# Pairs of column tiles of the input projection as seven products of halves, with sums of weights kept from the first block

## The chip, the core and the metric

The kernel runs on one core of one Trainium2 chip. The metric is the device time of one launch in microseconds. A core has TensorE (matmuls, PE in the rows; its weight loads are PEld), VectorE (DVE), ScalarE (ACT), GpSimd (POOL), and SyncE (SP), which here issues the DMAs. Each engine works through its own queue in order.

## What is computed

One layer of a decoder trunk on 2048 tokens of 1024 channels. The four branches read the same normalised rows `h` through one projection of 9992 columns:

```python
h = _rmsnorm(x, norm_pre)
cols = h @ w_in
(dn_qkv, dn_z, dn_b, dn_a, gm_uv, gm_z, sw_q, sw_k, sw_v, sw_z,
 xm_q, xm_z, gate_logits) = _split_cols(cols)
mem_kv = _rmsnorm(mem, norm_mem) @ w_mem_kv
y_a = _deltanet_branch(dn_qkv, dn_z, dn_b, dn_a, conv_w, a_log, dt_bias, dn_norm)
y_b = _spatial_gating_branch(gm_uv, gm_z, gm_norm, spatial_w, spatial_b)
y_c = _sliding_window_branch(sw_q, sw_k, sw_v, sw_z, sinks)
y_m = _memory_branch(xm_q, xm_z, mem_kv)
proj = jnp.einsum("btnc,ncd->btnd", jnp.stack([y_a, y_b, y_c, y_m], axis=2), w_up)
gates = jax.nn.sigmoid(gate_logits.reshape(B, T, N_BRANCH, D))
out = jnp.sum(gates * proj, axis=2) @ w_out
return x + _rmsnorm(out, norm_post)
```

## The kernel before

**Tiles.** The 2048 tokens go in four blocks of 512 (`NPASS` is 4, a block is a pass `p` of the main loop). A block's `h` is held transposed, channels on the partitions: `hhi` and `hlo`, each 8 row tiles of 128 channels by 512 tokens. To keep float32 precision every operand is split in two: `hi` is the value cast to the matmul's type, `lo` is the rest, and `mac3` (L258) adds hi·hi, lo·hi and hi·lo into PSUM, three matmuls per row tile.

**Projection.** `proj2` (L264) makes two column tiles of 128 columns for the 512 tokens of a block: for each half `j` of the 1024 channels `wunit` (L228) loads 128 x 1024 weights (512 KB), splits them in two halves of 128 x 512 (ScalarE casts `hi`, L249; VectorE or GpSimd subtracts `lo`, L250, by the list `ON_DVE` and a count of three), and 24 matmuls of 512 columns follow. Two PSUM banks of the four under the tag `mm` take the pair, and `done` reads each bank. The columns of one block are 37 such pairs: `dn` (delta net q, k, v; names dn0, dn1, dnv), `gu` and `gz`, `skv`, `sq` and `sz`, `xq` and `xz`, `az`, and 16 `gate` pairs. The values `gv` and the output `wo` go with tokens on the partitions (`tokmajor`).

**Gates and up-projections.** `gates_up` (L422) makes for each of four branches and four pairs the gate's pair, then two up-projections of 4 x 3 matmuls, and adds their product to `merged` (VectorE L454, GpSimd L455). Where `h` is 1024 channels, an up-projection has 512.

**Order.** The main loop runs a foreground generator (`fg`) and after each of its steps one step of each background generator in `bg`: the convolutions, the delta rule's chain (`dn_step`, `dn_scan`; two a block), the sliding-window attention (`branch_c`) and the memory attention (`branch_m`). The tile framework then orders each engine's queue and waits for buffers: 3 raw buffers of 512 KB (`NWR`), 6 pairs of split buffers of 128 x 512 (`NW`), 12 work tiles (`NT`). All weight loads, and the small stores and loads of the chain, are issued by SP.

## Time and profile before

| | |
|---|---|
| median of three runs | 2728.31 us (2728.02 to 2730.84) |
| profiled execution | 2728.63 us |
| its span, first to last instruction | 2726.9 us |
| mean granted TensorE clock | 0.994 |
| TensorE busy | 2684.6 us, 98% |
| VectorE busy | 1546.7 us, 57% |
| ScalarE busy | 1105.2 us, 41% |
| GpSimd busy | 682.2 us, 25% |
| moved by DMA | 271.29 MB, mean 99 GB/s |

The page gives for each engine the time in which it worked, its share of the span and the number of instructions; then the span in 40 slices; the DMA queues; the chain that ended last; and the costliest groups of instructions. A matmul's duration overlaps the next one's, so its price in a row of matmuls is read from start to start. Idle time of an engine is listed with what ended it.

### The profile page before, as it was taken

The numbers are of one execution on the slowest core, as the hardware profiler recorded it, in microseconds if no ns is written. First come the engines' busy times: TensorE is split into PE (matmuls) and PEld (weight loads), VectorE is DVE, ScalarE is ACT, GpSimd is POOL, SyncE is SP. The second block draws the span as 40 slices with busy tenths as digits, with TensorE's granted clock in tenths as the row PEclk, the third lists the DMA queues.
The fourth block names the chain that finished last, engine by engine and source line by source line (L and its number), as shares of the span: only waits on it lengthen the run. The fifth ranks groups of instructions, "written<-read, shape, count | busy, mean of one in ns | idle before, by whom it ended". The sixth has DMA issues, their size and how long they took to land. (4 is left out here: it accounts for less than half of the span.)

```text
span 2726.9 us, 37167 instructions
## 1 busy us (share of the span) xinstructions
PE 2684.6 (98%) x13453; PEld 2176.5 (80%) x13453; DVE 1546.7 (57%) x3355; ACT 1105.2 (41%) x2484; POOL 682.2 (25%) x689
## 2 busy tenths in 40 slices
PE   7989999999999999999999999999999999999998
PEld 5868777888888877888878887788887877778887
DVE  7464377544557547754465656665447455675444
ACT  5524343334453444343444334434344443433332
POOL 3333322011224332101223433210113334221111
PEclk9989999999999999999999999999999999999999
DMA  4342333224433233323533323332343332333242
GB/s 136 103 118 86 93 93 86 85 85 137 143 89 104 76 93 87 100 70 93 170 102 94 104 78 85 103 91 71 108 155 116 88 96 74 89 95 89 78 123 93
DMA packets 268015, 271.29 MB, mean 99 GB/s; under 512 B 33264, under 2 KB 238648, under 8 KB 267832
## 3 DMA queue, kind: packets, MB, share of 16 engines
q1 hardware_dynamic: 267656, 268.89, 34.1%
q8 instruction: 106, 1.74, 0.3%
q14 instruction: 77, 0.63, 0.1%
q10 hardware_dynamic: 80, 0.03, 0.0%
q0 software_dynamic: 96, 0.01, 0.0%
HBM read 251.31 MB, written 12.06 MB: 97 GB/s over the span
## 5 line engine op out<-in xcount | busy, mean ns | idle before, releaser
L455 POOL TENSOR_TENSOR merged<-merged,gp 128x512 f32<-128x512 f32 x96 | 138.7, 1445 | 685.2 <-DVE gp L454 670.4
L675 DVE TENSOR_TENSOR pr<-L,U 128x8 f32<-128x8 f32 (+31 forms) x256 | 102.0, 398 | 44.2 <-DMA L<-scr 37.4
L431 ACT ACTIVATE gt<-gate 128x512 f32<-128x512 f32 x128 | 76.2, 595 | 122.1 <-PE gate L262 121.8
L260 PE MATMUL gate<-hhi,gate1hi 128*128 128x512 f32 x256 | 105.9, 414 | 0.0
L260 PE MATMUL gate<-hhi,gate2hi 128*128 128x512 f32 x256 | 102.3, 400 | 0.0
L260 PE MATMUL wo<-wohi,mh 128*128 128x512 f32 x256 | 102.0, 399 | 0.0
L260 PE MATMUL gate<-hhi,gate3hi 128*128 128x512 f32 x256 | 100.8, 394 | 0.0
L261 PE MATMUL gate<-hlo,gate1hi 128*128 128x512 f32 x256 | 100.5, 393 | 0.0
L262 PE MATMUL gate<-hhi,gate1lo 128*128 128x512 f32 x256 | 100.5, 393 | 0.0
L262 PE MATMUL wo<-wohi,ml 128*128 128x512 f32 x256 | 100.0, 391 | 0.0
L261 PE MATMUL gate<-hlo,gate2hi 128*128 128x512 f32 x256 | 100.0, 391 | 0.0
L261 PE MATMUL gate<-hlo,gate3hi 128*128 128x512 f32 x256 | 100.0, 391 | 0.0
L260 PE MATMUL gate<-hhi,gate0hi 128*128 128x512 f32 x256 | 99.9, 390 | 0.0
L262 PE MATMUL gate<-hhi,gate2lo 128*128 128x512 f32 x256 | 99.9, 390 | 0.0
L262 PE MATMUL gate<-hhi,gate3lo 128*128 128x512 f32 x256 | 99.8, 390 | 0.0
L261 PE MATMUL wo<-wolo,mh 128*128 128x512 f32 x256 | 99.6, 389 | 0.0
L261 PE MATMUL gate<-hlo,gate0hi 128*128 128x512 f32 x256 | 99.6, 389 | 0.0
L262 PE MATMUL gate<-hhi,gate0lo 128*128 128x512 f32 x256 | 99.6, 389 | 0.0
L250 DVE TENSOR_TENSOR gate0lo<-gate0raw,gate0hi 128x512 fp32r<-128x512 f32 x64 | 44.0, 692 | 94.7 <-ACT gate0hi L249 94.7
L454 DVE SCALAR_TENSOR_TENSOR gp<-gt,up 128x512 f32<-128x512 f32 x96 | 65.6, 683 | 54.0 <-PE up L262 53.2
L250 POOL TENSOR_TENSOR gate1lo<-gate1raw,gate1hi 128x512 fp32r<-128x512 f32 x48 | 62.1, 1301 | 125.8 <-ACT gate1hi L249 125.7
L250 DVE TENSOR_TENSOR gate3lo<-gate3raw,gate3hi 128x512 fp32r<-128x512 f32 x64 | 44.3, 692 | 81.7 <-ACT gate3hi L249 81.7
(483 smaller groups left out, 8272.8 us busy)
## 6 DMA issues: line engine op xcount, KB each, us to landing
gate1raw<-in_w_in_dram SPq DMA_DIRECT2D x32, 512.0 KB, 3.6
gate2raw<-in_w_in_dram SPq DMA_DIRECT2D x32, 512.0 KB, 3.6
gate3raw<-in_w_in_dram SPq DMA_DIRECT2D x32, 512.0 KB, 3.6
gate0raw<-in_w_in_dram SPq DMA_DIRECT2D x32, 512.0 KB, 3.7
woraw<-in_w_out_dram SPq DMA_DIRECT2D x32, 512.0 KB, 3.8
xx<-in_x_dram SPq DMA_DIRECT2D x32, 256.0 KB, 5.1
dn0raw<-in_w_in_dram SPq DMA_DIRECT2D x16, 512.0 KB, 3.6
dn1raw<-in_w_in_dram SPq DMA_DIRECT2D x16, 512.0 KB, 3.7
```

The costliest lines, as they stand in the source:

```text
L250: ins = eng.tensor_tensor(lo, rw, hi.bitcast(F32), op=ALU.subtract)
L260: T.matmul(ps, lh, rh, start=first, stop=False)
L261: T.matmul(ps, lh, rl, start=False, stop=False)
L262: T.matmul(ps, ll, rh, start=False, stop=last)
L431: A.activation(t, ps, AF.Tanh, scale=0.5)
L454: V.scalar_tensor_tensor(g, ts[d2], 1.0, ps, op0=ALU.add, op1=ALU.mult)
L455: G.tensor_tensor(merged[:, d], merged[:, d], g, op=ALU.add)
L675: V.tensor_tensor(pv, L[:, i, i:32].unsqueeze(1).broadcast_to([P, 8, n]), U[:, :, i:32], op=ALU.mult)
```

## The change

In blocks 2 to 4 a pair of column tiles is no longer two sums over 1024 channels. Tokens, channels and columns are each halved: the 512 tokens in two halves of 256, the 1024 channels in two of 512, the 256 columns in two of 128. The four result quarters C11 to C22 come from seven products of halves (`PROD`) instead of eight, each 4 row tiles x 3 parts = 12 matmuls of 256 columns. Four of the seven use the weights' own quarters B11 to B22, three use sums T1 to T4 of them; on the side of the tokens, four quarters A of `h` or sums S1 to S4 are used. T3, T2, T1 and T4 are formed in block 1 by GpSimd for each of the 37 pairs and stored to DRAM by DMAs that ScalarE issues (`form`, `store`); later blocks load them like weights. S1 to S4 are formed once a block by `left_sums`, S1 in the place of `h`'s quarter A21 (`left_last`), for which the value projection `gv` and the small gates of the delta net run first. Between products ScalarE copies and VectorE adds 256 columns in PSUM (`quad`). `job` emits two such pairs, or a pair and an up-projection, in turn, product by product; `land` lets the last one finish alone.

Beside this: a weight piece is 128 x 512 with a raw buffer of its own (5 of 256 KB instead of 3 of 512 KB); in block 1 all subtractions are VectorE's; `NT` is 11; the tile `inv` shares the buffer of `L` and is cleared per chain; the gate's product is written over the gate; four matmuls at the start write the PSUM banks.

```diff
-    def wunit(src, name, k=4, swap=False, tags=None):
+    def wraw():
+        return wp.tile([P, 512], F32, name="raw", tag="wraw", bufs=NWR)
+
+    def wsplit(raw, name, tags=None):
...
+        eng = V if name in ON_DVE or nsplit[0] % 3 == 0 and not solving or not fast else G
+        A.copy(hi, raw)
+        ins = eng.tensor_tensor(lo, raw, hi.bitcast(F32), op=ALU.subtract)
...
+    PROD = (("C11", "A11", "B11"), ("C21", "S3", "T3"), ("C12", "S2", "T2"), ("C11", "A12", "B21"),
+            ("C12", "S1", "T1"), ("C21", "A22", "T4"), ("C12", "S4", "B22"))
+    tsum, left = {}, {}
+
+    def quad(parts, name, done):
+        pieces, c0 = {}, parts[0][0][1]
+
+        def get(i):
+            n = PROD[i][2]
+            if n[0] == "T":
+                raw = wraw()
+                nc.sync.dma_start(raw, tsum[n, c0])
+            else:
+                raw = wload(w_in, parts, int(n[1]) - 1, int(n[2]) - 1)
+            pieces[i] = [r3(t, 4) for t in wsplit(raw, name)]
+
+        get(0)
+        get(1)
+        yield
+        bank = [mm(name), mm(name)]
+        ps = {f"C{a + 1}{b + 1}": bank[b][:, a * 256:(a + 1) * 256] for a in range(2) for b in range(2)}
+        for i, (c, a, _) in enumerate(PROD):
+            if i + 2 < len(PROD):
+                get(i + 2)
+            hi, lo = pieces.pop(i)
+            ah, al = left[a]
+
+            with tc.issue_after(opened) if i == 1 else nullcontext():
+                for k in range(4):
+                    ins = mac3(ps[c], hi[:, k], lo[:, k], ah[:, k], al[:, k], i == 0 and k == 0, k == 3, i > 0)
+                    if i == 0 and k == 0:
+                        opened = ins
+            if i == 0:
+                A.copy(ps["C12"], ps["C11"])
+            elif i == 1:
+                p7 = etmp("p7")
+                A.copy(p7, ps["C21"])
+            elif i == 2:
+                u2 = etmp("u2")
+                A.copy(u2, ps["C12"])
+                V.tensor_tensor(ps["C21"], ps["C21"], u2, op=ALU.add)
+            elif i == 4:
+                V.tensor_tensor(ps["C22"], ps["C12"], p7, op=ALU.add)
+            elif i >= 5:
+                done(i - 5, bank[i - 5])
+            yield
...
+    def job(gen):
+        next(gen)
+        if flying:
+            old = flying.pop()
+            while next(old, "end") != "end":
+                if next(gen, "end") == "end":
+                    yield from old
+                    return
+                yield
+        else:
+            for _ in range(3):
+                next(gen)
+                yield
+        flying.append(gen)
...
+        def form(n, u, v):
+            raw[n] = tmp(n)
+            G.tensor_tensor(raw[n], raw[u], raw[v], op=ALU.subtract)
+            tsum[n, c0] = dp.tile([P, 512], F32, name="tsum", tag=f"tsum{n}{c0}", bufs=1)
+            store(tsum[n, c0], raw[n])
...
+    def left_sums():
+        s1 = []
+        for j in (0, 2):
+            js = slice(j, j + 2)
+            a = {}
+            for n in ("A21", "A22", "A11", "A12"):
+                h, l = left["S1" if n == "A21" else n]
+                a[n] = tmp("s1") if n == "A22" else ctmp("sa")
+                (G if n in ("A22", "A12") else V).tensor_tensor(r3(a[n], 2), h.bitcast(F32)[:, js], l.bitcast(F32)[:, js], op=ALU.add)
+            V.tensor_tensor(a["A22"], a["A21"], a["A22"], op=ALU.add)
+            V.tensor_tensor(a["A21"], a["A11"], a["A21"], op=ALU.subtract)
+            V.tensor_tensor(a["A11"], a["A22"], a["A11"], op=ALU.subtract)
+            V.tensor_tensor(a["A12"], a["A12"], a["A11"], op=ALU.subtract)
...
+        if p:
+            fast[:] = [True]
+            sums = start(left_sums())
+            b0 = fg(branch_b_v())
+            left_last(finished(sums))
         d0 = fg(dn_project(0, gt))
```

What this makes of the queues is shown at three places. The names of a matmul row are its result, then what streams, then what is loaded as weights; a number tells buffers apart. First TensorE in block 2, at the gates of the memory branch (`gate3` the gate, `up3` its up-projection). Before:

```order
L261 MATMUL gate3_11328<-hlo_140,gate3hi_11401 128x512
L262 MATMUL gate3_11328<-hhi_139,gate3lo_11402 128x512
L260 MATMUL up3_11489<-ymh_10154,u3hi_11481 128x512
L1056 MATMUL xo_11457<-xpT0_11377,mkv_9625 128x512
L1056 MATMUL xo_11457<-xpT1_11378,mkv_9625 128x512
L261 MATMUL up3_11489<-yml_10155,u3hi_11481 128x512
L262 MATMUL up3_11489<-ymh_10154,u3lo_11482 128x512
```

And now:

```order
L272 MATMUL gate3_14148<-hlo_139,gate3hi_14292 128x256
L273 MATMUL gate3_14148<-hhi_138,gate3lo_14293 128x256
L271 MATMUL up3_14368<-ymh_13391,u3hi_14339 128x512
L272 MATMUL up3_14368<-yml_13392,u3hi_14339 128x512
L273 MATMUL up3_14368<-ymh_13391,u3lo_14340 128x512
L271 MATMUL gate3_14149<-shi_140,gate3hi_14351 128x256
L272 MATMUL gate3_14149<-slo_141,gate3hi_14351 128x256
L273 MATMUL gate3_14149<-shi_140,gate3lo_14352 128x256
```

Before, all of a gate's pair stood ahead of its up-projection; now one row tile of the up-projection stands between two products of the next gate, and the products have 256 columns.

Second VectorE in block 2, where the convolutions of the second delta projection (`dn1a`) meet the subtractions for the memory queries (`xqlo`). Before:

```order
L250 TENSOR_TENSOR xqlo<-xqraw,xqhi 128x512
L542 SCALAR_TENSOR_TENSOR dn1a<-dn_9355,ccol,dn1a 128x511
L544 SCALAR_TENSOR_TENSOR dn1a<-carry,ccol,dn1a 128x1
L954 COPY_PREDICATED sc<-gt_mask,scp 128x2x128
L546 COPY carry<-dn_9355 128x3
L954 COPY_PREDICATED sc<-gt_mask,scp 128x2x128
L542 SCALAR_TENSOR_TENSOR dn1a<-dn_9356,ccol,dn1a 128x509
L544 SCALAR_TENSOR_TENSOR dn1a<-carry,ccol,dn1a 128x3
```

And now:

```order
L706 SCALAR_TENSOR_TENSOR dn1a<-dn_11161,ccol,dn1a 128x509
L708 SCALAR_TENSOR_TENSOR dn1a<-carry,ccol,dn1a 128x3
L244 TENSOR_TENSOR xqlo<-raw,xqhi 128x512
L706 SCALAR_TENSOR_TENSOR dn1a<-dn_11161,ccol,dn1a 128x510
L708 SCALAR_TENSOR_TENSOR dn1a<-carry,ccol,dn1a 128x2
L244 TENSOR_TENSOR xqlo<-raw,xqhi 128x512
L706 SCALAR_TENSOR_TENSOR dn1a<-dn_11161,ccol,dn1a 128x511
L708 SCALAR_TENSOR_TENSOR dn1a<-carry,ccol,dn1a 128x1
```

The subtractions have moved in between the operations of one convolution, one after each of its taps.

Third ScalarE at the start of block 1, where the first weights are cast (`dn0hi`) and `h` is written. Before:

```order
L249 CAST dn0hi<-dn0raw 128x512 x2
L476 CAST baw<-bar 128x8x8
L249 CAST dn0hi<-dn0raw 128x512
L346 ACTIVATE hhi<-xtp,ccol 128x512 x5
L249 CAST dn0hi<-dn0raw 128x512
L346 ACTIVATE hhi<-xtp,ccol 128x512 x3
```

And now:

```order
L243 CAST dn0hi<-raw 128x512 x2
L99 DMA tsum<-T_288 128x512
L640 CAST baw<-bar 128x8x8
L243 CAST dn0hi<-raw 128x512 x2
L99 DMA tsum<-T_354 128x512
L448 ACTIVATE hhi<-xtp,ccol 128x512 x5
L99 DMA tsum<-T_357 128x512
L448 ACTIVATE hhi<-xtp,ccol 128x512 x3
```

Stores of the sums (`tsum`), each of which waits for GpSimd's result, now stand ahead of the two parts of `h`.

## Rows read from the trace of the kernel before

**Rows 1.** The page: engines' busy time (share, instructions); TensorE's clock in 40 slices.

```profile
PE 2684.6 (98%) x13453; PEld 2176.5 (80%) x13453; DVE 1546.7 (57%) x3355; ACT 1105.2 (41%) x2484; POOL 682.2 (25%) x689
...
PEclk9989999999999999999999999999999999999999
```

**Rows 2.** Waits of TensorE: who waits for whom, us in total, times, longest.

```profile
PE xtp L342 <- DVE xx L328: 10.4, 3, 8.3
PE z L696 <- DMA lt<-scu: 6.3, 1, 6.3
PE gv L260 <- DVE dnva L544: 3.5, 4, 1.8
```

**Rows 3.** Busy time by stretch: block 2, then two tight stretches of it.

```profile
core 0: us, PE busy (x) PEld busy (x) DVE busy (x) ACT busy (x) POOL busy (x), PEclk, DMA share, GB/s
...
732.70:1395.40 662.70, 660.61 (x3323) 536.08 (x3322) 381.42 (x828) 271.56 (x612) 165.52 (x166) 1.00 0.35 100
...
997.50:1064.60 67.10, 67.10 (x317) 52.22 (x316) 47.98 (x117) 34.33 (x87) 17.00 (x14) 1.00 0.33 95
1064.60:1153.10 88.50, 87.12 (x507) 69.68 (x505) 63.56 (x144) 30.70 (x69) 18.74 (x22) 1.00 0.34 90
```

**Rows 4.** TensorE's timeline: first and last of 14 matmuls (start, duration, us).

```profile
439.03 0.39 PE L260 MATMUL gate<-hhi,gate2hi 128*128 128x512 f32 x1
...
441.98 0.39 PE L261 MATMUL gate<-hlo,gate2hi 128*128 128x512 f32 x1
```

**Rows 5.** The same at 256 columns: memory projection, and scores between up-projections.

```profile
153.15 0.28 PE L260 MATMUL mkps<-memT,mkpshi 128*128 128x256 f32 x1
...
154.81 0.28 PE L262 MATMUL mkps<-memT,mkpslo 128*128 128x256 f32 x1
...
430.32 0.28 PE L260 MATMUL xs<-mkh,xqh 128*128 128x256 f32 x1
...
431.04 0.40 PE L260 MATMUL up<-ych,u2hi 128*128 128x512 f32 x1
```

**Rows 6.** The tile mkpshi: its weight loads (ns, min/median/max).

```profile
L260 PEld LDWEIGHTS mkps<-memT,mkpshi x32: 186/192/192, 141.1 to 154.5; 128*128 128x128 f32 x32
```

**Rows 7.** Groups by line: casts and subtractions (busy us, mean ns | idle before).

```profile
L249 ACT CAST gate2hi<-gate2raw 128x512 fp32r<-128x512 f32 x64 | 39.4, 622 | 77.2 <-PE gate L261 49.8 <-PE xz L261 20.1 <-PE xq L261 5.4
...
L250 DVE TENSOR_TENSOR gate2lo<-gate2raw,gate2hi 128x512 fp32r<-128x512 f32 x64 | 43.6, 691 | 13.7 <-ACT gate2hi L249 10.5 <-PE ssp L576 2.7
...
L250 POOL TENSOR_TENSOR gate1lo<-gate1raw,gate1hi 128x512 fp32r<-128x512 f32 x48 | 62.1, 1301 | 125.8 <-ACT gate1hi L249 125.7
```

**Rows 8.** Operations of 256 columns from PSUM: a copy, a subtraction (min/median/max).

```profile
L1050 ACT COPY xpT<-xtp 128x256 f32<-128x256 f32 x64 | 21.1, 378 | 20.1 <-PE xtp L1047 16.4 <-PE pvo L988 3.7
...
L380 DVE TENSOR_TENSOR mkl<-mkps,mkh x4: 413/415/418, 154.2 to 165.2; 128x256 fp32r<-128x256 f32 x4
```

**Rows 9.** DMA: landing times; a stretch with 512-byte rows; SP's time per issue.

```profile
gate2raw<-in_w_in_dram SPq DMA_DIRECT2D x32, 512.0 KB, 3.6
...
sqraw<-in_w_in_dram SPq DMA_DIRECT2D x32, 256.0 KB, 3.1
...
974.00:997.50 23.50, 23.50 (x110) 18.81 (x109) 8.58 (x15) 9.27 (x18) 7.51 (x8) 1.00 0.41 112
...
L233 SPq DMA_DIRECT2D gate2raw<-in_w_in_dram x32: 367/380/398, 373.2 to 2440.2; - x32
```

**Rows 10.** Timelines of ScalarE and VectorE: a cast, and its subtraction.

```profile
1032.76 0.62 ACT L249 CAST xzhi<-xzraw 128x512 fp32r<-128x512 f32 x1 [0.37 <-PE dnv L261]
...
1042.34 0.68 DVE L250 TENSOR_TENSOR xzlo<-xzraw,xzhi 128x512 fp32r<-128x512 f32 x1
```

**Rows 11.** Groups by line: subtractions of the third gate.

```profile
L250 DVE TENSOR_TENSOR gate3lo<-gate3raw,gate3hi 128x512 fp32r<-128x512 f32 x64 | 44.3, 692 | 81.7 <-ACT gate3hi L249 81.7
```

**Rows 12.** Subtractions of the memory queries: min/median/max, then as a group (mean).

```profile
L250 DVE TENSOR_TENSOR xqlo<-xqraw,xqhi x32: 659/682/1775, 359.5 to 2473.0; 128x512 fp32r<-128x512 f32 x32
...
L250 DVE TENSOR_TENSOR xqlo<-xqraw,xqhi 128x512 fp32r<-128x512 f32 x32 | 25.8, 817 | 7.1 <-ACT xqhi L249 7.1
```

**Rows 13.** Waits of SP's queue.

```profile
SPq L661 <- POOL m L658: 75.5, 24, 5.2
```

More of the change, by code (lines that the diff above doesn't have):

```diff
@@ new lines, in trunk, with land, proj2 @@
+    flying = []
+    def job(gen):
[12 more added lines that the diff above has]
+        flying.append(gen)
+    def land():
+        while flying:
+            yield from flying.pop()
+    def proj2(parts, name, done, w=None, rh=None, rl=None, n=TB):
+        if fast:
+            yield from job(quad(parts, name, done))
+            return
@@ L395, in trunk @@
     V.memset(S, 0.0)
+    for i in range(4):
+        T.matmul(mm("init"), ident, S.rearrange("p h c -> p (h c)"), start=True, stop=True)
     carry = cp.tile([P, 12, 3], F32, name="carry")
@@ L595, in dn_step @@
         q, gt, ssp = st["q"], st["gt"], st["ssp"]
-        while any(g in bg for g in st["posts"] + [gt["gen"]]):
+        while len(st["posts"]) < 6 or any(g in bg for g in st["posts"] + [gt["gen"]]):
             yield
@@ L825, in branch_b @@
         yield
+        return (vs,)
+    def branch_b(vs):
         ys, mixes = [], []
@@ L900, in done @@
             start(values())
-        yield from proj2(cols_of(w_in, OFF_SK), "skv", done)
+        yield from proj2(cols_of(OFF_SK), "skv", done)
         return kph, kpl, vt
@@ L1058, in branch_m @@
         yield
+        while 2 not in ups_done:
+            yield
         ys[h] = ysplit(sz, "ym")
```

234 lines of the change are left out of this document (147 added, 87 removed).

## Prediction

> **What bounds the kernel now.** I read the page first, then the waits of TensorE, then the stretches of one block, then single matmuls. The page gives TensorE 2684.6 us of work in a span of 2726.9, with the granted clock at 90% of full speed or more in all but one of forty slices [rows 1]. Its waits are few, and the longest belong to the first microseconds, before the first block has its rows [rows 2]. One later block of 512 tokens takes 662.7 us and keeps TensorE busy for 660.6 of them; VectorE works for 381.4, ScalarE for 271.6, GpSimd for 165.5 [rows 3]. So the end is set by the number of matmuls and by their pitch, and the other engines have room on average. Durations overlap their successors, so I price a matmul by start to start: 13 steps from 439.03 to 441.98, 0.227 us for 512 columns [rows 4].
>
> The kernel's own time for the profiled execution is 2728.63 us, 1.7 more than the span, and the median of the runs is 2728.31. I sum against 2728.6 and read the result as that of the median. About 0.2% (5.5 us) is what a measurement of this kernel can tell from no change.
>
> **The matmuls.** Blocks 2 to 4 have 37 pairs of column tiles each (6 dn, 4 gu and gz, 1 skv, 4 sq and sz, 4 xq and xz, 2 az, 16 gate), 111 in all. A pair was 2 tiles x 8 row tiles x 3 parts = 48 matmuls of 512 columns, 48 x 0.227 = 10.90 us. It becomes 7 products x 4 x 3 = 84 matmuls of 256 columns. The trace has such matmuls, with the same type and the same three-part accumulation, in the memory projection: 14 steps from 153.15 to 154.81, 0.1186 us; six in the memory scores took 0.72, so 0.120 [rows 5]. A pair then costs 84 x 0.1186 = 9.96 or 84 x 0.120 = 10.08. The saving is 0.94 or 0.82 a pair, 104 or 91 us in all. I take 97, midway, since the new products stand between scores and transposes as often as in a long row. Columns alone fall by an eighth, 1.36 us a pair; what is lost of this is a fixed part. Two pitches of 0.1186 are 10 ns more than one of 227, and 36 matmuls are added.
>
> On this part a rule can be weighed against the rows: by the Trainium skill, "TensorE: Matmul & The Clock Gate", section "Back-to-back issue gap", a warm matmul takes its columns at 2.4 GHz and 2.5 ns. By that 256 columns would be 109 ns, a pair would save about 1.18 us and the change about 131 (an estimate from that page). The rows have four times that fixed part, and I stay with them.
>
> **What the other engines get.** A pair needs 7 pieces of weights of 128x512 instead of 4. Each is cast by ScalarE (0.622 us) and subtracted by VectorE (0.69) or GpSimd (1.30) [rows 7]. Counted in the built order, a block has 111 more casts, 82 more subtractions on VectorE and 32 more on GpSimd. Three copies and two additions of 256 columns between accumulators are added per pair; the nearest rows are 0.378 on ScalarE and 0.415 on VectorE [rows 8]. The sums of the left operand are, per block, about 20 VectorE, 8 ScalarE and 4 GpSimd operations of 512 columns. So VectorE: 381 + 82 x 0.69 + 74 x 0.42 + 20 x 0.69 = 483 us. ScalarE: 272 + 111 x 0.62 + 111 x 0.38 + 5 = 388. GpSimd: 166 + 32 x 1.3 + 5 + 2 for the cleared tile = 215. TensorE's block would be 662.7 - 37 x 0.87 = 630. On average everything is hidden: VectorE 77%, ScalarE 62%. In the tightest stretch, the second delta projection and the first memory queries, VectorE has 48.0 of 67.1 us [rows 3]; it gains some 10.4 while the stretch shrinks to 62.7, so 93%. In the second gate stretch it is 63.6 + 11.6 of 85, 88%. There cover is thin.
>
> **The wait that is added.** A piece now lives in one of 5 raw buffers of 256 KB, where there were 3 of 512 KB, and each of the 6 split buffers is used up in 12 matmuls, 1.42 us, where it was 2.73. A raw buffer is held from issue to the end of the subtraction: 3.1 us to land 256 KB [rows 9] + 0.62 + 0.69 = 4.4 us, plus any time W that the subtraction queues. Five buffers at 1.42 allow 7.1, so W may reach 2.7 us before TensorE starves; six halves at 2.73 allowed four times that. Where VectorE waits for the cast, as in the third gate (81.7 us of its idle time ends with the cast), W is nothing [rows 11]. After the second delta projection one cast began at 1032.76 and its subtraction at 1042.34: W is 9.0, while VectorE works on the convolutions of that projection [rows 10]. The excess there is 9.0 - 2.7 = 6.3 us. One such place a block gives 19 us in three blocks; this is the unknown with the widest ends, from 0 (the order in the changed kernel puts the subtractions between the convolutions) to 60 (three places a block). I take 19, as that row is the nearest.
>
> SP's queue carries the loads: some 7 issues of 0.38 us a pair instead of 2 [rows 9], 2.7 us in 10, so the queue itself suffices. It also carries the 16 small stores of a chain, and it waited 24 times for GpSimd's masks, 75.5 us in all, longest 5.2 [rows 13]. Loads behind such a wait come later by up to that, which the 7.1 us of the raw buffers absorb less well; this is inside the 0 to 60.
>
> The transfers: a pair moves 1.84 MB instead of 1.05, in rows of 512 bytes or 2 KB. The stretch with 512-byte rows moved 112 GB/s at 41% [rows 9], so the 150 GB/s of a later block (100 x 662.7 + 29 MB over 630) would fill about 55%. No limit.
>
> **Smaller terms.** Two jobs alternate so that a copy or an addition (0.4 us) has another job's product (1.42) as cover. That cover is gone where a job starts alone or is landed: twice a block, about 1 us each, 6 in all (0 to 12). The left sums run beside the value projection, which has been moved ahead of the delta projection; S1 overwrites part of h after the last use of h, and its first reader is the fifth product, so I put 1 us a block, 3 in all (0 to 9). Block 1 saves nothing: GpSimd forms 148 sums (148 x 1.3 = 192 us more, for 166 in a later block now), and ScalarE issues 148 stores, each of which waits for its sum with casts and h behind it. At the start one sum stands ahead of the row norms on GpSimd and one store ahead of h on ScalarE: 2 to 3 us. I take 7 for the block (-3, as pieces of 256 KB land 0.5 us earlier than those of 512 [rows 9], to 25).
>
> Sum: -97 + 19 + 6 + 3 + 7 = -62, so 2728.6 - 62 = 2666.6, **2667 us**.
>
> **Rivals.** *All is hidden.* Pitch 0.1186, no queueing above 2.7 us: -104 with 8 to 12 of start costs, 2633. For it: the order keeps most subtractions several products ahead of their use. Against it: W up to 9.0 at 71% VectorE load, and the load rises.
>
> *The raw buffers become the bound (slower).* In the 21 pairs a block that stand without up-projections between them, 441 pieces in three blocks, the pitch of a piece is (4.4 + W)/5. With 97 won and 16 of other costs, the gain is gone when these pieces lose 81/441 = 0.18 us each, that is at a mean W of 5 x 1.60 - 4.4 = 3.6 us. At 4.5 it is 1.78 a piece, 0.36 x 441 = 159 lost: 2728.6 - 97 + 16 + 159 = 2807. For it: the 9.0 above. Against it: W is nothing in the third gate, and VectorE's mean load stays at 77%.
>
> *VectorE and GpSimd exclude each other.* If no operation of the one ran beside one of the other, a block would need 483 + 215 = 698 us, 35 more than now: 2728.6 + 3 x 35 + 7 = 2841. Subtractions that took 682 ns in the median took up to 1775 [rows 12], so some do wait for GpSimd; but the mean over the xq pieces is 817 [rows 12], so most don't. The Trainium skill, "SBUF — State Buffer", section "SBUF: two separate sides", has this as a lock for VectorE operations with two SBUF inputs, and the row with 1775 agrees. A small chance.
>
> *The products aren't cheaper.* If the pitch at 256 columns were that of a weight load (0.19 us), a pair would cost 16 us and the kernel be far slower. The 0.1186 rows have just such loads, 192 ns each, hidden [rows 5, 6]. I give it almost nothing.
>
> **How the numbers follow.** Forecast, 2640 to 2705: 0.52. All hidden, 2622 to 2640: 0.18. The buffers take most of the gain, 2705 to 2723: 0.08. Within 0.2%: 0.05. Slower: 0.17, of which the raw buffers 0.12, the exclusion 0.04, the pitch 0.01. So faster 0.78, same 0.05, slower 0.17. The range reaches from -104 with next to no cost, 2622, to 2740, which leaves out the core of the slower rivals.
>
> **What would show it.** Products at 0.1186 to 0.120 in rows of twelve; a later block of about 640 us; VectorE near 480 in it; block 1 within 7 us of its old length. If the raw buffers bind, TensorE waits for subtractions of dn, xq, gu and gz pieces, and SP for them in turn. If exclusion rules, subtractions average well above 0.8 us. The forecast is wrong if these waits pass 90 us, or if block 1 alone grows by more than 25.

## The result and the profile after

The changed kernel takes 2874.15 us in the median of 3 runs (2871.73 to 2890.19) against 2728.31, a ratio of 1.0548 with an interval of 1.0488 to 1.0608. It is 146 us slower, where 62 us less were forecast.

The first part of the page after, to be read against [rows 1]: engine, busy us, share of the span (2872.4 us), instructions.

```profile
PE 2683.5 (93%) x17457; PEld 2350.7 (82%) x17457; DVE 1937.6 (67%) x3914; ACT 1395.2 (49%) x3116; POOL 975.8 (34%) x848
```

TensorE's busy time is what it was (2684.6), but it is busy for 93% of the span and not 98%. That the sum did not fall is an effect of how matmuls are drawn: those of 256 columns start 0.12 us apart and are shown 0.28 long. What they cost is read from start to start.

The four blocks by stretch, against [rows 3]. Columns: stretch, length, busy us of TensorE, its weight loads, VectorE, ScalarE and GpSimd with instructions, granted clock, the transfers' share, GB/s.

```profile
0.00:762.50 762.50, 713.95 (x3528) 575.58 (x3529) 477.52 (x944) 298.23 (x663) 316.33 (x274) 0.97 0.51 151
762.50:1466.00 703.50, 658.88 (x4656) 594.00 (x4655) 488.14 (x997) 369.43 (x829) 221.90 (x193) 0.97 0.49 135
1466.00:2168.80 702.80, 658.17 (x4655) 592.80 (x4654) 489.36 (x997) 369.79 (x828) 220.51 (x193) 0.98 0.49 136
2168.80:2872.40 703.60, 652.55 (x4623) 588.32 (x4622) 482.61 (x979) 357.79 (x801) 217.09 (x191) 0.98 0.47 132
```

Block 1 grew from 732.7 to 762.5 us, the later ones from 662.7, 662.1 and 669.4 to some 703. VectorE works for 488 us in block 2 (483 forecast), ScalarE for 369 (388), GpSimd for 222 (215). The loads came out as summed and no engine is full; the time went elsewhere.

To see where, I took each step from the start of one matmul to the start of the next, less the lower quartile of that step for its shape. What is over goes to the wait that the trace shows ahead of the second matmul; without one to the half clock, where the step lies in a stretch with a granted clock of 0.50 (1.2 GHz); and else to "rest". Us:

| | block 2 before | block 2 after | blocks 2 to 4, after less before |
|---|---|---|---|
| matmuls at their own pitch | 622.1 | 591.1 | -93.4 |
| waits for the steps between products | 0 | 29.3 | +86.9 |
| waits for a cast or subtraction of weights | 0 | 2.8 | +8.7 |
| other waits (chains, small transfers) | 2.9 | 21.0 | +53.7 |
| half clock | 0 | 14.5 | +36.0 |
| rest | 37.7 | 44.8 | +24.2 |
| length | 662.7 | 703.5 | +115.8 |

With block 1's 29.7 this is the 145.5 us by which the spans differ. The parts of the last column add up to 0.3 more than the length; the stretch behind the last matmul, which no such step covers, is that much shorter. The "steps" are the copies of lines 315, 318 and 321 on ScalarE and the additions of lines 322 and 324 on VectorE.

TensorE's waits after, against [rows 2]. Columns: what waited, what ended the wait: us in all, times, longest.

```profile
PE gate L271 <- DVE gate L322: 32.3, 15, 4.7
PE z L862 <- DMA lt<-scu: 14.1, 5, 6.0
PE gps L687 <- DVE g L681: 11.7, 3, 3.9
PE xq L271 <- ACT u L321: 8.0, 3, 2.7
PE xz L271 <- ACT xz L315: 7.6, 3, 2.5
PE sq L271 <- ACT sq L315: 7.3, 6, 2.0
...
PE gv L272 <- DVE gvlo L244: 5.2, 4, 1.5
```

Waits for subtractions, the forecast's main risk, are far down the list (gvlo). The steps make the largest part of the list, led by the addition of line 322.

**One such wait.** The first gate stretch of block 2 holds the longest, 4.71 us. First TensorE, in order of time (start, us, instruction, and in brackets the idle time ahead of it with what ended it); then ScalarE, VectorE and GpSimd.

```profile
930.84 0.28 PE L273 MATMUL gate<-hhi,gate1lo 128*128 128x256 f32 x1
935.83 0.58 PE L271 MATMUL gate<-hhi,gate1hi 128*128 128x256 f32 x1 [4.71 <-DVE gate L322]
936.20 0.42 PE L272 MATMUL gate<-hlo,gate1hi 128*128 128x256 f32 x1
936.42 0.41 PE L273 MATMUL gate<-hhi,gate1lo 128*128 128x256 f32 x1
936.63 0.41 PE L271 MATMUL gate<-hhi,gate1hi 128*128 128x256 f32 x1
```
```profile
930.39 0.37 ACT L321 COPY u<-gate 128x256 f32<-128x256 f32 x1
...
934.32 0.36 ACT L315 COPY gate<-gate 128x256 f32<-128x256 f32 x1 [2.62 <-DVE szs L554]
```
```profile
928.12 0.20 DVE L839 TENSOR_TENSOR pr<-L,U 128x40 f32<-128x40 f32 x1
...
928.47 0.68 DVE L1068 COPY kpv<-svt 128x512 f32<-128x512 f32 x1
929.07 0.61 DVE L839 TENSOR_TENSOR pr<-L,U 128x48 f32<-128x48 f32 x1
929.60 1.35 DVE L1069 COPY vc<-kpv 128x128 f32<-128x128 f32 x1
...
931.09 1.07 DVE L839 TENSOR_TENSOR pr<-L,U 128x56 f32<-128x56 f32 x1
...
932.44 0.95 DVE L839 TENSOR_TENSOR pr<-L,U 128x64 f32<-128x64 f32 x1
...
933.56 0.68 DVE L554 SCALAR_TENSOR_TENSOR szs<-szt,sz 128x512 f32<-128x512 f32 x1
...
934.92 0.24 DVE L839 TENSOR_TENSOR pr<-L,U 128x80 f32<-128x80 f32 x1
...
935.35 0.42 DVE L322 TENSOR_TENSOR gate<-gate,u 128x256 f32<-128x256 f32 x1
```
```profile
928.31 6.22 POOL L244 TENSOR_TENSOR gate1lo<-raw,gate1hi 128x512 fp32r<-128x512 f32 x5 [2.44 <-DMA raw<-tsum]
```

ScalarE has the copy of line 321 ready at 930.76. The addition that takes it starts at 935.35, because VectorE works through its list in order and has a triangular solve ahead of it. That list crawls: a product of 128x40 took 0.20 us at 928.12 and 0.61 to 1.07 us for 128x48 to 128x64 from 929.07 on, and a copy of 128x128 took 1.35. In the same time GpSimd makes five subtractions without a pause, 928.31 to 934.53, and behind them 128x80 takes 0.24 again. The operations with an operand in an accumulator (kpv and szs, 0.68 both) aren't slower there. Against the short times around them VectorE's operations lose some 3.4 us in this burst, by an estimate from these rows and those between them: most of this wait.

The product that waits is the fourth of its job. It writes C11, not C21, which line 322 adds to; but both lie in one accumulator of 512 columns. In the compiled program the fourth product waits for line 322 of its own job in 108 of 111 jobs, the second for the copy of line 315, made right behind the first, in all 111, the fifth for line 321 in 111, the seventh for line 324 in 105. The Trainium skill, "PSUM — Partial Sum Buffer", section "PSUM bank collisions raise a hardware error", asks for just this: waits by bank, not by address, whenever two engines touch one. So ahead of the fourth product stand two steps on two engines in a row, and here the other job covers them with one product of 1.44 us.

**The clock.** The same place and two more, by stretch (the granted clock is the last number but two):

```profile
797.20:807.40 10.20, 7.03 (x31) 6.76 (x32) 3.29 (x18) 7.90 (x17) 2.92 (x4) 0.50 0.17 43
921.50:931.00 9.50, 9.44 (x78) 9.15 (x77) 5.80 (x17) 6.01 (x12) 6.48 (x6) 1.00 0.83 236
933.70:940.50 6.80, 4.67 (x22) 4.68 (x23) 5.10 (x18) 0.97 (x2) 2.06 (x2) 0.50 0.35 109
```

From 921.5 to 931.0 TensorE worked for 9.44 of 9.50 us at the full 2.4 GHz. Inside its 4.71 us of waiting the clock fell to 1.2 GHz and came back at 940.5. Till then a step of 256 columns takes 0.21 to 0.22 us (936.20, 936.42, 936.63) and not 0.12. The other stretch, from 797.2, begins in a wait of 3.91 us at the start of the block. There were 3 such stretches before and 28 after.

### The profile page after: what moved, and what is told of

It reads as the page before. It is cut to its first block, busy times and chain, and to the rows that moved or that the text cites. A ratio compares the mean times of both kernels' runs of the same rounds, so it can differ in the third digit from the quotient of the medians.

```text
span 2872.4 us, 49476 instructions
## 1 busy us (share of the span) xinstructions
PE 2683.5 (93%) x17457; PEld 2350.7 (82%) x17457; DVE 1937.6 (67%) x3914; ACT 1395.2 (49%) x3116; POOL 975.8 (34%) x848
## 5 line engine op out<-in xcount | busy, mean ns | idle before, releaser
L599 POOL TENSOR_TENSOR merged<-merged,gt 128x512 f32<-128x512 f32 x96 | 141.0, 1471 | 657.4 <-DVE gt L598 630.7
L362 POOL TENSOR_TENSOR T<-raw 128x512 f32<-128x512 f32 x74 | 103.5, 1408 | 98.6 <-DMA raw<-in_w_in_dram 68.4
L244 POOL TENSOR_TENSOR gate1lo<-raw,gate1hi 128x512 fp32r<-128x512 f32 x69 | 88.0, 1290 | 79.0 <-ACT gate1hi L243 65.0
L244 DVE TENSOR_TENSOR gate0lo<-raw,gate0hi 128x512 fp32r<-128x512 f32 x100 | 77.8, 781 | 53.9 <-ACT gate0hi L243 53.2
L362 POOL TENSOR_TENSOR T<-raw,T 128x512 f32<-128x512 f32 x74 | 105.4, 1425 | 15.1 <-issue 6.8
L271 PE MATMUL gate<-hhi,gate1hi 128*128 128x256 f32 (+1 forms) x256 | 86.6, 338 | 20.3 <-DVE gate L322 20.3
L271 PE MATMUL gate<-hhi,gate2hi 128*128 128x256 f32 (+1 forms) x256 | 83.8, 327 | 11.4 <-DVE gate L322 11.4
L273 PE MATMUL gate<-hhi,gate1lo 128*128 128x256 f32 (+1 forms) x256 | 83.8, 330 | 0.4 <-POOL gate1lo L244 0.4
L272 PE MATMUL gate<-hlo,gate1hi 128*128 128x256 f32 (+1 forms) x256 | 83.8, 327 | 0.0
L271 PE MATMUL gate<-hhi,gate0hi 128*128 128x256 f32 (+1 forms) x256 | 80.7, 315 | 2.7 <-ACT u L321 2.1
```

The lines of the kernel that those rows point to most:

```text
L244: ins = eng.tensor_tensor(lo, raw, hi.bitcast(F32), op=ALU.subtract)
L271: ins = T.matmul(ps, lh, rh, start=first, stop=False, skip_group_check=more)
L272: T.matmul(ps, lh, rl, start=False, stop=False, skip_group_check=more)
L273: T.matmul(ps, ll, rh, start=False, stop=last, skip_group_check=more)
L362: G.tensor_tensor(raw[n], raw[u], raw[v], op=ALU.subtract)
L599: G.tensor_tensor(merged[:, d], merged[:, d], t, op=ALU.add)
```

## The experiments

Theory A: TensorE waits for the steps between products, which are late in their engines' lists, and the half clock follows such waits. Its rivals: the raw buffers and subtractions bind (theory B, the prediction's); the load on VectorE and ScalarE as such; VectorE and GpSimd exclude each other. For block 1: the sums and stores (theory C), or the smaller pieces.

All kernels are the changed one but for the edit shown, if nothing else is said. The medians of the kernel before in the same sets were 2727.9 to 2730.3 us.

### Steps between products

```diff
...
-            if i == 0:
-                A.copy(ps["C12"], ps["C11"])
...
-                V.tensor_tensor(ps["C22"], ps["C12"], p7, op=ALU.add)
-            elif i >= 5:
+            if i >= 5:
```


> Blocks 2 to 4 without the five steps between products (three copies of 256 columns on ScalarE, two additions on VectorE); each product goes to its own quarter, so the outputs lack those sums. Pieces, matmuls and transfers are those of the changed kernel. Theory A: TensorE loses about 29 us a block directly at these steps (waits on the lines 315, 321 and 322), and some 10 us a block of half clock behind such waits; then a later block falls from 703 to about 663, and the kernel from 2874 to about 2755 (2725 to 2785). Theory B, the raw buffers and the subtractions bind: the pieces are the same, so a block stays within 10 us of 703 and the kernel above 2840.

Measured: 2792.24 us, 82 less, outside the ranges of both theories. Block 2 lasts 677.0: the 29.3 of waits at the steps are gone, and the "rest" falls from 44.8 to 34.8, so that shorter waits at the steps may have been part of it; but waits for casts and subtractions rise from 2.8 to 13.1, and the half clock takes 16.4. The first half of theory A holds; that the clock would recover with it does not. TensorE has a new wait of several us, three times some 5.5:

```profile
PE gate L271 <- ACT gate1hi L243: 16.6, 3, 6.1
```

It stands in the gate stretch above. ScalarE, in block 2:

```profile
950.32 0.40 ACT L1127 ACTIVATE sc<-sc,cnm 128x128 f32<-128x128 f32 x1 [9.44 <-DVE cnm L1121]
...
952.44 2.17 ACT L243 CAST gate1hi<-raw 128x512 fp32r<-128x512 f32 x4
```

ScalarE is not full there. It stands idle for 9.44 us for a small operation of the attention (cnm), which has the triangular solve ahead of it in VectorE's list, and the casts of the gate's weights stand behind in ScalarE's own.

```diff
...
-                A.copy(ps["C12"], ps["C11"])
+                A.copy(etmp("p7"), bsb[:, 0:256])
...
-                V.tensor_tensor(ps["C22"], ps["C12"], p7, op=ALU.add)
+                V.tensor_tensor(etmp("u2"), bsb[:, 0:256], bsb[:, 256:512], op=ALU.add)
```


> As the run without the five steps, but ScalarE and VectorE still make three copies and two additions of 256 columns a pair, on constants that nobody writes, and TensorE waits for none of them; the outputs lack the sums. If the loss is TensorE's waiting for these steps (theory A), this kernel is within 20 us of the one without them, about 2765. If it is the load that they put on ScalarE (41 us a block) and VectorE (31 us a block), it is near the changed kernel, 2850 to 2875.

Measured: 2822.21 us. Of the 82 us, 52 are TensorE's waiting for the steps and 30 the load that they put on ScalarE and VectorE. Neither of the two forecasts was right by itself. The 30 is rather too much for the steps' load: these additions have both operands in SBUF and averaged 0.52 and 0.68 us, up to 1.53, where the real ones, with an operand in an accumulator, averaged 0.42 and 0.43.

```diff
...
+    PROD = (("C11", "A11", "B11"), ("C21", "S3", "T3"), ("C12", "S2", "T2"), ("C21", "A22", "T4"),
+            ("C11", "A12", "B21"), ("C12", "S1", "T1"), ("C12", "S4", "B22"))
...
-        ps = {f"C{a + 1}{b + 1}": bank[b][:, a * 256:(a + 1) * 256] ...
+        ps = {f"C{a + 1}{b + 1}": bank[1 - a][:, b * 256:(b + 1) * 256] ...
...
```


> The quarters that a copy ties together (C11 and C12) share one 512-column accumulator and C21 and C22 the other, and the product of A22 stands fourth; the number of steps, matmuls and pieces is the same, the outputs are not (rows and columns of quarters change places). In the changed kernel the second product of a job waits for the copy behind the first, and the fourth for a copy and an addition behind the third; here only one product waits for a single step right ahead of it. Theory A: of the 29 us a block of waits at these steps 12 to 20 go, with some half clock, so a block falls to 680 to 690 and the kernel to 2800 to 2840. If the load of the steps on ScalarE and VectorE makes the loss, it stays at 2860 to 2880.

Measured: 2840.31 us, 34 less, at the edge of what theory A gave. In block 2 the waits at the steps fall only from 29.3 to 24.9, where theory A took 12 to 20 off; the half clock falls from 14.5 to 7.7. Fewer products wait right behind a step, but a step that is late by 4 us is late for the next product too. By this, one product more of distance does little against a list that is several us late.

### Raw buffers, the start of a block, block 1

```diff
-NW, NWR = 6, 5
+NW, NWR = 6, 4
```


> Four raw buffers of 256 KB in place of five, all else as in the changed kernel. If the raw buffers bind (the rival of the prediction), a piece's least pitch rises by a quarter and the later blocks, whose pieces number 259 each, grow by 20 us or more: kernel above 2930. If they have room, as the few waits for subtractions say, blocks grow by less than 6 us and the kernel stays within 2870 to 2895.

Measured: 2903.41 us, between the two, 29 more. The profiled execution took 23 more, 9 in block 1 and 5, 0 and 9 in the others. Five buffers weren't the bound, but there is no slack to speak of below them.

```diff
-            sums = start(left_sums())
-            b0 = fg(branch_b_v())
-            left_last(finished(sums))
+            if p == 1:
+                sums = start(left_sums())
+            if p < 3:
+                b0 = fg(branch_b_v())
...
```


> Block 2 is that of the changed kernel. Blocks 3 and 4 make no left sums (they read those of block 2, so the outputs are wrong), and block 4 has its value projection back behind the delta projection, after landing the job in flight. In the changed kernel the first 60 us of each later block lose some 9 us to waits and 5 to half clock. If the left sums make these, blocks 3 and 4 are 8 to 14 us shorter than block 2 (703). If the place of the value projection makes them, block 3 stays near 700 and block 4 falls to about 690. If neither does, all three stay near 703.

Measured: 2878.63 us; blocks 2 to 4 last 702.2, 700.0 and 712.5. Without left sums block 3 is 2 us shorter than block 2, and block 4 isn't shorter with the value projection in its old place. That is one execution, and in two other runs, with four forms and with four stores, the same last block took 703 and 710 us; so the 712.5 say little. No sign that a block's start is slow for either reason.

```diff
...
-            if w is None:
+            if w is None and not tsum.get("full"):
                 for t in ...
```


> Only the first pair of block 1 forms and stores its four sums; all pairs of blocks 2 to 4 load these four in place of their own, so the outputs are wrong and the transfers of the later blocks the same. Block 1 lasted 762.5 us in the changed kernel and 732.7 before. Theory C, the 148 sums on GpSimd and 148 stores from ScalarE make the 30 us: block 1 falls to about 735 and the kernel to 2846. If block 1 is long for other reasons (pieces of 256 KB in five buffers, all subtractions on VectorE), block 1 stays near 760 and the kernel at 2870. Later blocks stay at 703 by both.

Measured: 2841.20 us. Block 1 falls to 726.2, the others stay (703.2, 706.4, 703.4). The 148 sums and stores are all of block 1's loss and more, 36 us.

```diff
...
-            tsum[n, c0] = dp.tile(...)
-            store(tsum[n, c0], raw[n])
+            if n not in tsum:
+                tsum[n] = dp.tile(...)
+                store(tsum[n], raw[n])
```


> Block 1 forms all 148 sums on GpSimd but stores only four; the later blocks load these four, so the outputs are wrong. Block 1 lasted 762.6 us with all sums and stores and 726.2 with four of each. If the sums' work on GpSimd (209 us) makes block 1 long, it stays above 755 and the kernel at 2868 to 2876. If the stores on ScalarE's queue, each of which waits for its sum with casts behind it, make it, block 1 falls to 726 to 735 and the kernel to 2840 to 2848.

Measured: 2864.43 us, 10 less, and block 1 at 741.9, between the two forecasts. By block 1 the stores make 20.6 of the 36.3 us and the sums 15.7; that the kernel gained only 10 is that its later blocks were 1 to 6 us longer, with 17 to 18 us of half clock each. Why these differed isn't settled.

### Splitting weights, and GpSimd

```diff
-        eng = V if name in ON_DVE or nsplit[0] % 3 == 0 and not solving or not fast else G
+        eng = V if name in ON_DVE or True else G
```


> All subtractions of weights stand on VectorE, none on GpSimd, in blocks 2 to 4 too; the outputs stay what they were. Theory of exclusion (VectorE and GpSimd lock each other out, and that makes the copies and additions late): GpSimd's subtractions are gone, so blocks fall by 10 us or more, kernel below 2845. Theory A (steps between products are late because their engine's queue is full): VectorE gets some 50 more operations of 0.69 us a block ahead of the additions, so blocks grow by 0 to 15 us, kernel 2875 to 2920.

Measured: 2843.83 us, 30 less, with more work on the busier engine: block 2 has 509 us of VectorE for 488, and lasts 689.5. Theory A by itself forecast the wrong sign. Either GpSimd's results came late, or GpSimd holds up VectorE. The traces show both. VectorE's time above the tenth percentile of each form of instruction (counting operations more than 15% above it) falls from 231 us in the changed kernel to 156. And ScalarE's idle time that ends with a result of GpSimd falls from 164 to 109 (VectorE's from 66 to 61).

```diff
...
         ins = eng.tensor_tensor(lo, raw, hi.bitcast(F32), op=ALU.subtract)
+        if not (name in ON_DVE or nsplit[0] % 3 == 0 and not solving or not fast):
+            for c in range(4):
+                tc.keep_in_program_order(
+                    G.tensor_tensor(dump, bsb[:, c * P:c * P + P], bsb[:, 384 - c * P:512 - c * P], op=ALU.subtract))
```


> All subtractions of weights on VectorE, as in the run that took 2844 us; and in GpSimd's order, where the changed kernel had its 240 subtractions of blocks 2 to 4, stand four subtractions of 128 columns each, on constants, into a tile that nobody reads. If GpSimd's work holds up VectorE while it runs (exclusion), the gain of 30 us goes again: 2865 to 2890, and VectorE's time over the shortest of each form rises from 156 us to above 210. If GpSimd's subtractions cost time because their results came late, it stays at 2835 to 2852.

Measured: 3011.33 us, 167 more than without this work, for which nobody waits. Its size (min, median, max ns), and TensorE's waits:

```profile
L250 POOL TENSOR_TENSOR dump<-bsb x960: 449/462/1122, 807.8 to 2636.0; 128x128 f32<-128x128 f32 x192
```
```profile
PE ssp L745 <- ACT sqh L742: 31.3, 3, 10.6
PE sq L277 <- DVE sq L328: 29.3, 5, 9.6
PE sq L277 <- ACT sq L321: 24.8, 6, 7.9
```

It is 443 us of GpSimd, where the 240 subtractions were 312 (240 x 1.30), and it comes in denser bursts. But these three waits don't show an exclusion. What stands ahead of the longest of the first kind, on GpSimd and then on ScalarE; and on VectorE, ahead of the longest of the third kind and of the second:

```profile
821.72 19.87 POOL L250 TENSOR_TENSOR dump<-bsb 128x128 f32<-128x128 f32 x33
841.54 1.04 POOL L739 TENSOR_TENSOR sq<-dn0a 128x512 f32<-128x512 f32 x1
```
```profile
842.62 0.62 ACT L742 CAST sqh<-sq 128x512 fp32r<-128x512 f32 x1 [12.01 <-POOL sq L739]
```
```profile
921.94 0.87 DVE L1028 TENSOR_TENSOR gs<-gs,gzs 128x512 f32<-128x512 f32 x1 [7.28 <-POOL gzs L1026]
...
1078.46 0.67 DVE L960 TENSOR_TENSOR on<-on,or 128x256 f32<-128x256 f32 x1 [9.05 <-POOL or L958]
```

Nobody waits for the added work, but results of GpSimd that others do wait for (sq, gzs, or) stand behind it in GpSimd's list. ScalarE and VectorE are idle for them, and the steps of the products behind that. VectorE's time above the tenth percentile rises from 156 to 204, not above 210 as forecast. So this run can't tell the two apart. It shows that late results of GpSimd can cost much: the nine longest waits of these kinds, three a block, make 84 us against the 167. That the exclusion exists is shown in the last section, from single operations. How the 30 us of the run before divide between the two stays open.

```diff
...
             if n[0] == "T":
-                raw = wraw()
-                nc.sync.dma_start(raw, tsum[n])
+                nc.sync.dma_start(hi.bitcast(F32), tsum[n])
+                nc.sync.dma_start(lo.bitcast(F32), tsum[n])
...
```


> As the run with four forms (2841 us), and the pieces of sums are loaded twice, as high and as low part, and neither cast nor subtracted: per block 148 casts and 148 subtractions fewer, 38 MB more to load; the outputs are wrong. The steps between products are all there. If the load of splitting on ScalarE, VectorE and GpSimd is what makes the steps and the chains late, the waits at the steps fall from 29 to under 15 us a block and the half clock with them: blocks near 665, kernel near 2720 (2690 to 2760). If the steps cost TensorE time by their own latency, blocks stay above 690 and the kernel above 2800.

This edit stands on the kernel with four forms (2841.20). Measured: 2756.42 us, 85 less. Block 2 at 674.5 has 17.0 us of waits at the steps for 29.3 (under 15 were forecast), 14.1 of other waits for 21.0 and 7.5 of half clock for 14.5, though its transfers fill 0.67 for 0.49. The load of splitting drives all three.

### Changes together

The edits of the runs with four forms, with all subtractions on VectorE and with the other pairing, in one kernel:

> Three single changes together: four forms (33 us less than the changed kernel alone), all subtractions on VectorE (30 less), the other order and pairing of the quarters (34 less); the outputs are wrong. If these are separate losses they add up: 2874 - 97 = 2777 (2765 to 2790). If the subtractions on GpSimd and the pairing cure the same waits, less than 20 of the second 64 us come on top: 2795 to 2810.

Measured: 2772.96 us. Four forms, no subtractions on GpSimd and the other pairing add up (33, 30 and 34 from 2874 give 2777).

The edits of the runs with four forms, with all subtractions on VectorE and without steps, in one kernel:

> Four forms, no steps between products, all subtractions on VectorE; pieces, matmuls and transfers of the later blocks as in the changed kernel; the outputs are wrong. From single runs: 2874 - 82 - 33 = 2759, and up to 31 less if what GpSimd's subtractions cost is apart from the steps: 2728 to 2759. If matmuls alone then set the end it would be 2728.6 - 97 = 2632 or little above. Above 2720 the products don't pay even with steps and sums for nothing.

Measured: 2717.83 us, below the 2728 to 2759 forecast and 0.4% below the kernel before (ratio 0.9961, 0.9949 to 0.9973). With sums, stores and steps for nothing the products win 11 us of the 97. Block 2 lasts 663.6: its matmuls take 593.0, and there remain 22.6 of waits and 11.0 of half clock that the kernel before hasn't.

### Pairs of 512 columns

The first of these stands on the kernel with four forms:

```diff
...
-            fast[:] = [True]
-            sums = start(left_sums())
+            later[:] = [True]
             b0 = fg(branch_b_v())
-            left_last(finished(sums))
...
-        eng = V if name in ON_DVE or nsplit[0] % 3 == 0 and not solving or not fast else G
+        eng = V if name in ON_DVE or nsplit[0] % 3 == 0 and not solving or not later else G
```


> All four blocks in pairs of 512 columns, four sums formed in all, no left sums; the value projection stays ahead of the delta projection, and pieces of 256 KB in five raw buffers and the smaller edits stay. If all of the loss of the later blocks lies in the products and what they need, a block is back at 662 us, block 1 near 733, and the kernel at 2728 within 10. If the pieces or the moved value projection cost time by themselves, blocks are 5 to 15 us longer and the kernel is at 2745 to 2775.

Measured: 2720.61 us (ratio 0.9970, 0.9959 to 0.9981), a later block 663.1, 661.7 and 667.9. All of the later blocks' loss lies in the products and what they need.

Then the same without the four sums:

```diff
-            if w is None and not tsum.get("full"):
-                for t in ...
-                    form(*t)
```


> All blocks in pairs of 512 columns, no sums of weights or of h at all; of the change there remain pieces of 256 KB in five raw buffers, all subtractions of block 1 on VectorE, the value projection ahead of the delta projection from block 2 on, and the smaller edits. The run with four sums in block 1 took 2720.6 us against 2727.9 of the kernel before, all of it in block 1 (725.5 for 732.9). The same here: 2717 to 2722. If the four sums and stores cost time, up to 2 us less; if the 7 us were a chance of one run, 2726 to 2730.

Measured: 2721.88 us (0.9967, 0.9954 to 0.9979). Four sums cost nothing that shows.

On this kernel stand the next two:

```diff
-        eng = V if name in ON_DVE or nsplit[0] % 3 == 0 and not solving or not later else G
+        eng = V if name in ON_DVE or nsplit[0] % 3 == 0 and not solving else G
```


> The kernel of pairs without sums, with GpSimd's share of the subtractions in block 1 again, as the kernel before had it. Block 1 was 721.5 us without that share and 732.9 in the kernel before. If that share makes the difference, block 1 is back at 730 to 734 and the kernel at 2727 to 2731; if the smaller pieces and buffers make it, block 1 stays near 722 and the kernel at 2720 to 2724.

Measured: 2724.88 us (0.9991, 0.9981 to 1.0000), between the two forecasts. By the medians GpSimd's share of the subtractions makes 3.0 of the 6.2 us by which the kernel without it was below the one before. Block 1, at 729.9 for 721.5, would give it more, but that compares one execution of each.

```diff
-        eng = V if name in ON_DVE or nsplit[0] % 3 == 0 and not solving or not later else G
+        eng = V if name in ON_DVE or True else G
```


> The kernel of pairs without sums (2721.9 us), with GpSimd's subtractions of blocks 2 to 4 on VectorE too. Those blocks have few waits (2 us) and almost no half clock, and VectorE stands at 57%: no change, 2717 to 2724. If GpSimd's subtractions cost here too, 2 to 6 us less a block would be seen: 2705 to 2716.

Measured: 2709.05 us (0.9928, 0.9916 to 0.9940), the best of all, and not what I expected: the later blocks had 2 us of waits, and yet lose 2 to 5 us.

```profile
PE 2682.2 (99%) x13461; PEld 2177.7 (80%) x13461; DVE 1604.3 (59%) x3539; ACT 1106.6 (41%) x2432; POOL 406.7 (15%) x448
```
```profile
722.60:1382.90 660.30, 659.84 (x3324) 536.50 (x3323) 396.03 (x872) 273.02 (x600) 99.94 (x108) 1.00 0.38 100
```
```profile
PE cps L190 <- DMA crow<-in_conv_w_dram: 7.2, 1, 7.2
PE z L859 <- DMA lt<-scu: 3.9, 1, 3.9
...
PE xo L1230 <- DMA mkv<-mvs: 0.8, 2, 0.5
```

Block 2 is at 660.3 us, and TensorE's longest wait in it is 0.28 us.

In the kernel before:

```diff
-            eng = V if name in ON_DVE or nsplit[0] % 3 == 0 and not solving else G
+            eng = V
```


> The kernel before with one line changed: all subtractions of weights on VectorE, none on GpSimd. The kernel of pairs took 2721.9 with GpSimd's subtractions in the later blocks and 2709.1 without. If GpSimd's subtractions are what costs there, the kernel before gains the same: 2706 to 2716, of which 7 to 11 in block 1. If the smaller pieces and buffers are needed for it, it stays above 2720.

Measured: 2711.80 us (0.9937, 0.9924 to 0.9951). One line in the kernel before is worth 16.5 us; the smaller pieces and buffers add 3 at most. In the profiled executions block 1 has 12.7 of it (732.7 to 720.0), where 7 to 11 were forecast. VectorE's time above the tenth percentile falls from 122 to 70 us, its idle time that ends with GpSimd stays (74 to 75), and ScalarE's falls from 87 to 65.

And in the kernel of pairs at 2709.05:

```diff
-                            G.tensor_tensor(merged[:, d], merged[:, d], t, op=ALU.add)
+                            V.tensor_tensor(merged[:, d], merged[:, d], t, op=ALU.add)
```


> The kernel of pairs with all subtractions on VectorE (2709.1), and the 96 additions of gates to the merged tile (1.47 us each on GpSimd, 141 us) on VectorE too, at about 0.69 us. TensorE is at 99% there with under 1 us a block of waits, so little is left: 2704 to 2710. If VectorE's own time became short, waits for up-projections' buffers would come back: 2712 to 2720.

Measured: 2709.52 us, the same as without it.

## Why the prediction was wrong

**The matmuls were right.** 31 us a block were saved at the matmuls' own pitch, 93.4 in all, for 97 forecast; the loads of the engines were right within 5%. The direction failed on what was put beside them.

**The steps between products were the mis-sized term.** The prediction took a copy or addition of 0.4 us as hidden under another job's product of 1.42, at nothing, and put 6 us (0 to 12) for the places where a job starts alone or is landed. TensorE's waits for the steps were 87 us, and leaving the steps out won 82. Two things were left out, both to be seen ahead of any run. A step waits in its engine's list behind work that itself waits; I asked that of the subtractions (the W of 9.0 us, [rows 10]) and not of the steps, which have less distance to their reader: between a job's first and second product, with the copy of line 315 between them, the built order has less than 1.4 us of other matmuls in 45 of 111 jobs. And two halves of one accumulator count as one for waits, so that the fourth product hangs on a chain of two steps.

**"On average everything is hidden" was the wrong test.** VectorE's 67% left room for the sum, not for each operation at its time. The chains of the recurrence and the attention wait for it too, and TensorE takes matmuls in a fixed order: 54 us that had no term.

**The clock had no term.** [Rows 1] showed it nearly constant, in a kernel whose TensorE hardly waited. 76 us' worth of full-speed work was lost to it in all, 17 before. By the table this is 36 us in blocks 2 to 4; in block 1 it is 20.5 for 11.0.

**Raw buffers were over-priced.** 19 us (0 to 60) were put in; the waits for casts and subtractions are 8.7. The rival that made them the bound falls: one buffer less cost 29 us, where it had 159 (0.36 us a piece) with all five.

**Block 1 was 30 us longer for 7** (bound 25): 36 from sums and stores, against 7 gained by the rest of the change there; by the run with the old split, at least half of those 7 by the subtractions that moved to VectorE.

**The exclusion was set aside too soon.** I priced it as all or nothing (2841) and gave it 0.04, since most subtractions weren't slow. It need not be complete: it is enough that a burst of GpSimd stretches VectorE's list in front of a step, as at 929 us. The sign that I named for it, subtractions well above 0.8 us in the mean, looked at the wrong operations: they average 0.77, and 0.74 before. Taking GpSimd's subtractions away gave 30 us of the 146, and 16.5 in the kernel before, so that the base of my sum held some of this already. How much of either is exclusion and how much late results of GpSimd, which had no price in the prediction, isn't separated.

The whole is no sum of separate causes: the steps cost 82 us with the splitting load there, and the splitting of the sums 85 with the steps there. The run without steps, with four sums and with all subtractions on VectorE shows the limit. Against the kernel of pairs with all subtractions on VectorE too, at 2709, its 2718 are still 9 us more: in this staging, where seven pieces are split for four, seven products don't pay even without the sums of weights and the steps.

## What to carry to other kernels

When matmuls are traded for small steps on other engines between them, price each step as a wait: how far its reader stands behind it, what else is in that engine's list, and which accumulator its operands share. Utilization of the other engines says nothing on this. And look at the clock behind a wait: here the two long ones shown were each followed by a stretch at 1.2 GHz. Before splitting elementwise work between VectorE and GpSimd, try it all on VectorE: here this one line gave 0.6%. And ask what else stands in GpSimd's list behind the work that is moved there.

## What the hardware showed that was not expected

GpSimd's operations on SBUF hold up VectorE's, short ones too. In the burst above, a product with two operands in SBUF went from 0.20 us to between 0.61 and 1.07, and a copy of 128x128 took 1.35, where the one in block 1, beside no GpSimd operation, took 0.23. Operations that read an accumulator kept their 0.68, and so did the short reductions of the solve theirs, some 0.2. Two groups of VectorE's operations in the changed kernel (min, median, max ns):

```profile
L954 DVE TENSOR_TENSOR on<-on,or x32: 424/426/1510, 220.4 to 2647.4; 128x256 f32<-128x256 f32 x32
```
```profile
L322 DVE TENSOR_TENSOR gate<-gate,u x48: 414/424/433, 935.3 to 2801.1; 128x256 f32<-128x256 f32 x48
```

Line 954 has all its operands in SBUF. Beside 22 of its 32 operations GpSimd had no operation with two operands, and they took 0.42 to 0.43 us; beside the other ten it had one, and they took 0.73 to 1.51. Line 322 reads an accumulator: of its 111 additions 35 ran beside such an operation, and all took 0.41 to 0.43. So the steps themselves aren't held up, but what stands ahead of them is.

The Trainium skill, "SBUF — State Buffer", section "SBUF: two separate sides", calls this an exclusive lock for the whole instruction, against VectorE's operations with two SBUF inputs or in a two-port mode. For two inputs the rows agree; whether the copy is in such a mode no run here shows. I had weighed that section in the prediction against means of long operations, where it shows least.

The solve's product shows it over the kernel (256 operations: min, median, max ns), in the order before, after, pairs with all subtractions on VectorE:

```profile
L675 DVE TENSOR_TENSOR pr<-L,U x256: 161/338/1425, 136.2 to 2455.1; 128x8 f32<-128x8 f32 x8, 128x24 f32<-128x24 f32 x8, 128x40 f32<-128x40 f32 x8, 128x56 f32<-128x56 f32 x8
```
```profile
L839 DVE TENSOR_TENSOR pr<-L,U x256: 171/326/1427, 152.4 to 2606.8; 128x8 f32<-128x8 f32 x8, 128x24 f32<-128x24 f32 x8, 128x40 f32<-128x40 f32 x8, 128x56 f32<-128x56 f32 x8
```
```profile
L836 DVE TENSOR_TENSOR pr<-L,U x256: 168/301/953, 136.2 to 2432.5; 128x8 f32<-128x8 f32 x8, 128x24 f32<-128x24 f32 x8, 128x40 f32<-128x40 f32 x8, 128x56 f32<-128x56 f32 x8
```

The longest, of 1.43 us, are in the kernel before as in the changed one; they end at 0.95 without GpSimd's subtractions.
